# First expert pair gathered alone from unsplit rows, filler matmuls in the norms and the route, and the router's logits in another order

## The chip, the cores and the metric

The kernel runs on one core of a Trainium2 chip. The metric is device time in microseconds (us) of one launch. TensorE (PE) multiplies, PEld is its weight loading, VectorE (DVE), ScalarE (ACT) and GpSimd (POOL) do the rest, and SyncE (SP) issues the weight DMAs. TensorE's clock has two levels, 1.2 and 2.4 GHz; the profile gives it as the granted clock, 0.50 and 1.00.

## The reference

Two transformer blocks follow one another on 256 tokens of 1024 features, all in float32. The first has two layers, each a mixer, a layer norm, a mixture of experts (MoE) and a layer norm. The second is a state-space and attention mixer and a large expert lookup. The change lies around the MoE of the first block and in the norms.

```python
def grouped_moe(h, router_w, router_b, w_gate, w_up, w_down):
    logits = t @ router_w + router_b
    ...
    sel_group = jnp.argmax(group_score, axis=-1)
    ...
    top_val, top_idx = lax.top_k(masked, TOP_K)
    top_w = jax.nn.softmax(top_val, axis=-1)
    combine = jnp.sum(jax.nn.one_hot(top_idx, N_EXPERTS) * top_w[..., None], axis=1)
    for e in range(N_EXPERTS):
        hidden = jax.nn.silu(t @ w_gate[e]) * (t @ w_up[e])
        out = out + combine[:, e:e + 1] * (hidden @ w_down[e])

def first_block(...):
    for i in range(DEPTH):            # 2 layers
        ...
        x = layer_norm(ALPHA * x + (1.0 + gate) * mixer(h), ...)
        ...
        x = layer_norm(ALPHA * x + (1.0 + gate) * grouped_moe(h, ...), ...)
```

## The kernel before

Tokens lie in two tiles of 128 rows (t = 0 and 1). All matmuls go through `mm` (line 163) and all transposes through line 187, so PE's rows carry those two lines. A float32 number can be split into a rounded part and a rest (`split`, lines 151 and 153), two tiles of the type fp32r; products of split numbers are three fp32r matmuls.

A norm (`layer_norm`) works tile by tile: DVE multiplies the mixer's result by its gate (L314), adds the residual and sums (L316), ACT makes mean and variance (L320, L324, L327), POOL the inverse root (L330), and DVE normalises (L335). `warm` puts filler matmuls on PE: float32, 128x128, result unused, each reading a tile of the norm or the route, so that it runs when that tile is written. Their numbers are in the table `WA`.

A MoE follows. `logits` transposes the normalised rows in four blocks of 128 columns at a time, copies them out of PSUM (half on DVE, L194, half on ACT, L196) and multiplies them by the router's weights; a product trails its transposes by two steps (`LAG`). Both parts of `split` of the rows (fp32r) are made after each tile is normalised. `route` is a chain of some 30 small DVE operations from the logits `r_L` (L584) to the selection `r_sel` (L637); six small matmuls count and rank the selected tokens, and `hots` (L666) turns ranks into 0/1 matrices. `moe_rest` then reads the highest count into a register of every engine and branches (L828): the body runs only if an expert has more than 64 tokens. Behind the branch `moe_gather` picks, with matmuls on the split rows (two parts, two tiles, eight blocks: 32 matmuls of 256 columns), the rows of four experts, that is of two pairs; ACT and DVE scale and shift them (L767, L769). Then comes the loop over eight pairs of experts: gate and up (64 matmul records, two experts side by side), the hidden product (L730, L731), four transposes, down, and the weighted scatter into `y`. Pairs 0 and 1 are gathered in front of the loop, the next two each time in the pairs 1, 3 and 5. For each pair the `m_dT` and `m_sw` work (two transposes, two matmuls with `r_cmb`) prepares the scatter.

Weights come in pieces of 1 MB over SP's queue into 15 buffers: 12 of the streams `w` and `hl`, 3 of the pool `a`, which also holds the normalised rows and their split parts. 14 loads stand in front of the split and the 15th behind it.

What runs in which order on an engine is set by the scheduler of the tile framework; `issue_after` pins an instruction behind another.

The second block starts with `normed`: ACT squares and sums `x_mid` (L1006), DVE and POOL make the inverse root, DVE writes it on a diagonal (`rms_diag`, L1013), and 16 matmuls transpose and scale the rows.

Of the kernel before, what the change touches and what calls it, by code (L numbers as in the profile page):

```python
# [8 lines left out]
F32 = mybir.dt.float32  # L9
# [33 lines left out]
WA = {4: 3, 5: 3, 6: 3, 7: 3, (2, 0): 1, (3, 0): 3}  # L43
LAG = 2
ATR = 4
# [9 lines left out]
class Net:  # L55
# [116 lines left out]
    def warm(self, src, n=1):  # L172

        if n == 0:
            return
        pt = self.psum()
        w = src.shape[1]
        if w < WN:
            src = src[:, None, :].to_broadcast([P, WN // w, w])
            pt = pt[:, :WN].rearrange("p (a w) -> p a w", w=w)  # L180
        else:
            src, pt = src[:, :WN], pt[:, :WN]
        for _ in range(n):
            self.mm(pt, self.ones, src, True, True)
# [119 lines left out]
    def layer_norm(self, x, y, i, j):  # L304
# [4 lines left out]
        xh = self.act8().rearrange("p (t d) -> p t d", t=T)  # L309
        for t in range(T):  # L310
# [27 lines left out]
        return xh  # L338

# [220 lines left out]
    def logits(self, xh):  # L560
# [26 lines left out]
    def route(self, L):  # L587
# [61 lines left out]
        first = self.hots(0, pos)  # L649
# [12 lines left out]
    def hots(self, pr, pos):  # L662

        dt = self.t2(512, F32R).rearrange("p (t e s) -> p t e s", t=T, e=4)
        for t in range(T):
            self.nc.vector.tensor_tensor(dt[:, t], self.iota128[:, None, :CAP].to_broadcast([P, 4, CAP]),  # L666
                                         pos[:, t, 2 * pr:2 * pr + 4, None].to_broadcast([P, 4, CAP]), op=OP.is_equal)
        return [dt[:, t].rearrange("p e s -> p (e s)") for t in range(T)]

    def moe(self, i, xh, sc, sh):  # L670
        nc, V = self.nc, self.nc.vector
        L = self.logits(xh)
# [26 lines left out]
        y = self.out_tiles()  # L699
        for t in range(T):  # L700
            for hf in range(2):
                self.mm(y[t][hf].rearrange("p (a w) -> p a w", a=4), self.zerob,
                        self.zerob[:, None].to_broadcast([P, 4, P]), True, False)
# [8 lines left out]
        first = self.moe_gather(xh, sc, sh, hot, cmb, 0)  # L712
        self.phase(f"moe{i}")
        one = self.wk.tile([P, 1], F32, name="m_one", bufs=1)
        nc.scalar.activation(one, cmb[:, 0, 0:1], AF.Silu)
        xg, dT, sw = first.pop(0)
        nxt, late = first, None
        for pr in range(8):
# [46 lines left out]
    def modulate_slots(self, eng, out, in_, sc, sh, k):  # L765
        if eng == "s":
            self.nc.scalar.activation(out, in_, AF.Identity, scale=sc[:, k:k + 1], bias=sh[:, k:k + 1])  # L767
        else:
            self.nc.vector.tensor_scalar(out, in_, sc[:, k:k + 1], sh[:, k:k + 1], op0=OP.mult, op1=OP.add)  # L769

    def moe_gather(self, xh, sc, sh, d, cmb, pr):


        nc = self.nc
        xg = [self.t4().rearrange("p (k s) -> p k s", k=KB) for _ in range(2)]
        for k2 in range(KB // 2):
# [3 lines left out]
            for q in range(2):  # L780
                for kk in range(2):
                    k = 2 * k2 + kk
                    self.modulate_slots("vs"[k2 % 2], xg[q][:, k], pg[:, kk, q * P:q * P + P], sc, sh, k)
        out = []
        for q in range(2):
            dT = self.wk.tile([P, T, 128], F32R, name="m_dT", bufs=3)
            sw = self.wk.tile([P, 1], F32, name="m_sw", bufs=3)
            pw = self.psum()
            dq = [d[t][:, q * P:q * P + P].bitcast(F32) for t in range(T)]
            es = slice(2 * (pr + q), 2 * (pr + q) + 2)  # L790
            for t in range(T):
                self.transpose(pw[:, t * P:t * P + P], dq[t])
            for t in range(T):
                self.mm(pw[:, 2 * P:2 * P + 2], dq[t], cmb[:, t, es], t == 0, t == 1)
            self.evac(dT, pw[:, :2 * P].rearrange("p (t s) -> p t s", t=T))
            for e in range(2):
                r = slice(64 * e, 64 * e + 64)
                nc.vector.tensor_copy(sw[r], pw[r, 2 * P + e:2 * P + e + 1])
            out.append((xg[q], dT, sw))
        return out  # L800

    def rest_gather(self, xh, sc, sh, d, w, xg, dT, ps):

        xg = xg.rearrange("p (k s) -> p k s", k=KB)
        for half in range(2):
            pg = ps[half].rearrange("p (k s) -> p k s", k=4)
            for kk in range(4):
                self.picked(pg[:, kk], xh, half * 4 + kk, d)
# [15 lines left out]
    def moe_rest(self, xh, sc, sh, cmb, pos, cnt, w, y):  # L824

        nc, tc, V = self.nc, self.tc, self.nc.vector
        most = nc.values_load(cnt[0:1, 16:17], min_val=0, max_val=S)
        with tc.If(most > CAP):  # L828
# [5 lines left out]
            dr = self.t2(S, F32R)  # L834
# [5 lines left out]
            with tc.For_i(0, 16, 1) as e:  # L840
# [6 lines left out]
                for base in (CAP, CAP + P):  # L847
                    with tc.If(have > base):
                        for t in range(T):
                            V.tensor_scalar(d[t], self.iota128, float(base), me[:, 0, t], op0=OP.add, op1=OP.is_equal)  # L850
                            V.tensor_scalar(dw[t], d[t].bitcast(F32), me[:, 1, t], None, op0=OP.mult)
# [147 lines left out]
    def normed(self, x, gcol, hl=None):  # L999
# [878 lines left out]
```

## Time and profile before

| | us |
|---|---|
| median of three runs | 2074.36 (2067.89 to 2075.95) |
| the profiled execution, its own time | 2072.57 |
| its span, first to last instruction | 2070.8 |
| PE busy in it | 1958.4 (95%) |
| DVE, ACT, POOL busy | 1206.9, 802.1, 410.5 |

The profile gives busy time per engine, a chain of work followed back from the last instruction, and, for any stretch, the instructions in order of time. In a row of that last view the columns are start, duration, engine, line, operation, output and inputs, shape, count, and in brackets the idle time of the engine in front of it and what ended it. A float32 matmul leaves two MATMUL records (the eight products of a tile read x16), an fp32r matmul one.

### The profile page before, as it was taken

Reading aid. Unit: us, or ns where it says so; the run is one execution under the profiler, and the core shown is the slowest. Engines: PE = TensorE matmul, PEld = TensorE weight load, DVE = VectorE, ACT = ScalarE, POOL = GpSimd, SP = SyncE. Lnnn points to the kernel's source line nnn. Section 1 sums busy time; section 2 is a strip of 40 time slices with the busy share of each in tenths; the row PEclk is TensorE's granted clock in tenths of the full one; section 3 lists DMA queues with packets and bytes.
Section 4 is the critical chain, followed back from the end, with each engine's and each line's share of the span. In section 5 each row is a group of like instructions: output and inputs, shape, how many; then the busy total and the mean of one; then the engine's idle time right before and its main releaser. Section 6 shows DMA issues by size and latency. Waiting matters only on the chain.

```text
span 2070.8 us, 31874 instructions
## 1 busy us (share of the span) xinstructions
PE 1958.4 (95%) x12566; PEld 1527.3 (74%) x12567; DVE 1206.9 (58%) x2489; ACT 802.1 (39%) x1254; POOL 410.5 (20%) x319
## 2 busy tenths in 40 slices
PE   6999999989999999987988999999999999999998
PEld 4967543438898844434766889999999998888886
DVE  3554321129895422104687569767999986555555
ACT  3344111124454311113433553555444445444444
POOL 1000000002232000000231134544665550000000
PEclk9999899999999999998998999999999999999999
DMA  9797699998875699996332361544564446555564
GB/s 388 284 405 269 253 393 394 394 390 284 304 271 187 245 365 394 395 391 263 138 116 88 114 257 32 163 143 143 163 194 154 145 151 193 193 194 193 194 194 151
DMA packets 155887, 496.09 MB, mean 240 GB/s; under 512 B 10176, under 2 KB 10592, under 8 KB 147152
## 3 DMA queue, kind: packets, MB, share of 16 engines
q1 hardware_dynamic: 152880, 483.42, 65.1%
q0 software_dynamic: 2848, 10.53, 1.4%
q8 instruction: 102, 1.67, 0.3%
q14 instruction: 57, 0.47, 0.1%
HBM read 486.30 MB, written 7.61 MB: 239 GB/s over the span
## 4 chain that ended last, share of the span: by engine, by line
PE 72%; DVE 10%; ACT 2%; issue 2%; DMA 2%; POOL 1%; POOLq 0%; SPq 0%; DVEq 0%; ACTq 0%
PE ps L163 42%; PE y L163 28%; DMA w<-moe_w_down 1%; DVE pair L1553 1%; PE y L1206 1%; DVE i L1454 1%; PE ps L187 1%; DVE et L1477 1%; DVE hl L153 1%; DVE pos L1465 1%; DVE v L1453 1%; ACT hl L151 0%; DMA raw<-s_tab 0%; DVE big L1561 0%; DVE cand L1460 0%
## 5 line engine op out<-in xcount | busy, mean ns | idle before, releaser
L163 PE MATMUL ps<-hn,pair 128*128 128x256 f32 x3072 | 383.5, 285 | 4.2 <-DVE pair L1553 4.1
L163 PEld LDWEIGHTS ps<-hn,pair 128*128 128x128 f32 x3072 | 373.8, 192 | 5.6 <-DVE pair L1553 5.1
L163 PE MATMUL y<-pair,hn 128*128 128x512 f32 x1512 | 342.9, 389 | 0.0
L163 PEld LDWEIGHTS y<-pair,hn 128*128 128x128 f32 x1512 | 283.8, 188 | 59.0
L163 PE MATMUL ps<-w,t 128*64 128x512 f32 x624 | 277.3, 595 | 8.7 <-DMA w<-moe_w_down 2.8
L163 PE MATMUL ps<-hl,t 128*64 128x512 f32 x624 | 278.4, 596 | 4.5 <-DVE t L194 3.1
L1553 POOL TENSOR_TENSOR pair<-raw,pair 128x640 fp32r<-128x640 f32 x128 | 235.2, 1845 | 158.0 <-ACT pair L1551 151.8
L153 DVE TENSOR_TENSOR pair<-raw,pair 128x1024 fp32r<-128x1024 f32 x128 | 156.7, 1225 | 147.1 <-ACT pair L151 147.1
L151 ACT CAST hl<-w 128x2048 fp32r<-128x2048 f32 x79 | 150.2, 1903 | 136.6 <-PE ps L163 77.1
L151 ACT CAST pair<-raw 128x1024 fp32r<-128x1024 f32 x128 | 135.0, 1055 | 172.7 <-PE y L163 171.6
L163 PEld LDWEIGHTS ps<-w,t 128*64 128x64 f32 x624 | 81.6, 137 | 117.2 <-issue 103.8
L1551 ACT CAST pair<-raw 128x1024 fp32r<-128x1024 f32 x128 | 134.2, 1051 | 65.7 <-PE ps L163 23.9
L153 DVE TENSOR_TENSOR hl<-w,hl 128x2048 fp32r<-128x2048 f32 x51 | 119.2, 2337 | 54.2 <-ACT hl L151 51.1
L163 PE MATMUL ps<-hl,a 128*128 128x256 f32 x1008 | 129.7, 287 | 1.8 <-ACT hl L151 1.8
L163 PEld LDWEIGHTS ps<-hl,t 128*64 128x64 f32 x624 | 81.1, 137 | 67.6 <-issue 60.7
L163 PEld LDWEIGHTS ps<-hl,a 128*128 128x128 f32 x1008 | 123.9, 191 | 5.7 <-ACT hl L151 2.0
L330 POOL TENSOR_TENSOR ln_st<-ln_st,c_mhalf 128x1 f32<-128x1 f32 x8 | 6.1, 768 | 605.3 <-ACT ln_st L327 605.2
L731 DVE TENSOR_TENSOR t<-t,ps 128x512 f32<-128x512 f32 x16 | 11.0, 688 | 171.8 <-PE ps L163 171.8
L163 PE MATMUL ps<-a,hl 128*128 128x256 f32 x864 | 105.7, 284 | 1.2 <-DVE a L153 1.2
L163 PEld LDWEIGHTS ps<-a,hl 128*128 128x128 f32 x864 | 104.2, 192 | 2.6 <-DVE a L153 1.4
L163 PE MATMUL ps<-a,t 128*64 128x512 f32 (+1 forms) x352 | 100.2, 537 | 1.4 <-ACT t L196 1.4
L747 DVE SCALAR_TENSOR_TENSOR t<-ps,m_sw,t 128x512 fp32r<-128x512 f32 x32 | 24.0, 750 | 132.5 <-ACT t L746 132.0
(431 smaller groups left out, 2886.5 us busy)
## 6 DMA issues: line engine op xcount, KB each, us to landing
raw<-peer_u SPq DMA_DIRECT2D x128, 512.0 KB, 3.4
raw<-peer_v SPq DMA_DIRECT2D x128, 512.0 KB, 3.4
w<-ada_w SPq DMA_DIRECT2D x35, 1024.0 KB, 7.5
w<-moe_w_down SPq DMA_DIRECT2D x28, 1024.0 KB, 14.3
hl<-moe_w_down SPq DMA_DIRECT2D x28, 1024.0 KB, 14.2
w<-moe_w_up SPq DMA_DIRECT2D x26, 1024.0 KB, 14.2
hl<-moe_w_up SPq DMA_DIRECT2D x26, 1024.0 KB, 14.3
w<-moe_w_gate SPq DMA_DIRECT2D x24, 1024.0 KB, 14.7
```

What stands on the lines that cost most here:

```text
L151: nc.scalar.copy(hi, src)
L153: nc.vector.tensor_tensor(lo, src, hi.bitcast(F32), op=OP.subtract)
L163: self.last_mm = self.nc.tensor.matmul(out, lhsT=lhsT, rhs=rhs, start=start, stop=stop, skip_group_check=True)
L187: self.nc.tensor.transpose(out, in_, self.ident[:in_.shape[0], :in_.shape[0]])
L747: V.scalar_tensor_tensor(yl[hf], py, sw, yh[hf].bitcast(F32), op0=OP.mult, op1=OP.subtract)
L1206: self.nc.tensor.matmul(py[32 * q:32 * q + 32, :S], lhsT=self.s5_ct[ct][:, 4 * i + q], rhs=ab[q % 2][:, x, ri], start=j == 0, stop=j == 3, ...
L1453: V.max(v[:, a, rs], s)
L1454: V.max_index(ix[:, a, rs], v[:, a, rs], s)
L1465: V.max_index(pos[:, 2, rs], top[:, h, rs], cd)
L1477: V.tensor_reduce(et[:, 0:2, h], oh.rearrange("p a k j -> p a j k"), axis=AX.X, op=OP.add)
L1551: nc.scalar.copy(up[:, 0], ur)
L1553: lo = eng.tensor_tensor(up[:, 1, ks], ur[:, ks], up[:, 0, ks].bitcast(F32), op=OP.subtract)
```

## The change

`logits` finishes both products of tile 0, and puts three zeroing matmuls of `y` behind them, ahead of the transposes of tile 1. The split of the normalised rows no longer stands between the norm and the route: it is pinned behind the last scaling of the first gather, and with it the 15th weight load. The first gather takes one pair alone, with 16 float32 matmuls of 128 columns on the unsplit rows; its `m_dT` and `m_sw` work stands behind gate and up of pair 0. The other pairs are gathered two at a time in the pairs 0, 2 and 4, and pair 7 alone in pair 6, still as 32 matmuls each. The read of the count on DVE is pinned behind the 0/1 matrices. Fillers are added at the start of each norm (4 in front of a MoE, 8 behind one), behind the logits (3), in the route (5, 5, 5, 3 in place of 3 each), behind the branch (3), in the norms on the squared tile (6 in place of 3), in the last norm (6 and 4) and in `normed` (4 and 5). A filler now holds the identity (`c_pack`) and streams the tile.

```diff
-WA = {4: 3, 5: 3, 6: 3, 7: 3, (2, 0): 1, (3, 0): 3}
+WA = {4: 5, 5: 5, 6: 5, 7: 3, (2, 0): 1, (3, 0): 6}
+FILL = {"norm": (4, 8), "L": 3, "pos": 3, "x": (6, 4), "xs": (4, 5)}
+GATHER = {0: (1, (0, 1)), 2: (3, (0, 1)), 4: (5, (0, 1)), 6: (6, (1,))}
...
         for _ in range(n):
-            self.mm(pt, self.ones, src, True, True)
+            self.mm(pt, self.ident, src, True, True)
+    def fill(self, src, n):
+        with self.tc.issue_after(self.last_mm.ins):
+            self.warm(src, n)
...
     def layer_norm(self, x, y, i, j):
+        self.fill(self.ones, FILL["norm"][j])
...
             if last:
+                self.warm(x[:, t], FILL["x"][t])
...
     def logits(self, xh, idle):
-                for k in range(4):
-                    self.transpose(pt[:, k], xh[:, t, (4 * q + k) * P:(4 * q + k + 1) * P])
+                with self.tc.issue_after(self.last_mm.ins):
+                    for k in range(4):
+                        self.transpose(pt[:, k], xh[:, t, (4 * q + k) * P:(4 * q + k + 1) * P])
...
+            while late and t == 0:
+                product()
+            if t == 0:
+                with self.tc.issue_after(self.last_mm.ins):
+                    idle()
         while late:
             product()
+        self.fill(h.rearrange("p k s -> p (k s)"), FILL["L"])
...
-        first = self.hots(0, pos)
+        first = self.hots(0, pos, 2, F32)
...
     def moe(self, i, xh, sc, sh):
-        for t in range(T):
-            self.split(hl[0][:, t], hl[1][:, t], xh[:, t])
-        xh = hl
-        load()
         cmb, pos, cnt, hot = self.route(L)
...
-        first = self.moe_gather(xh, sc, sh, hot, cmb, 0)
+        self.warm(self.ones, FILL["pos"])
+        xg, got = self.first_gather(xh, sc, sh, hot)
+        with self.after(*got):
+            for t in range(T):
+                self.split(hl[0][:, t], hl[1][:, t], xh[:, t], 512)
+        xh, nxt, late = hl, [], None
+        load()
...
+            if pr == 0:
+                dT, sw = self.moe_slots(hot, cmb, 0)
-            if pr % 2 and pr + 1 < 8:
-                nxt = self.moe_gather(xh, sc, sh, self.hots(pr + 1, pos), cmb, pr + 1)
+            if pr in GATHER:
+                b, qs = GATHER[pr]
+                nxt = self.moe_gather(xh, sc, sh, self.hots(b, pos), cmb, b, qs)
...
+    def first_gather(self, x, sc, sh, d):
+        xg, last = self.t4().rearrange("p (k s) -> p k s", k=KB), [None, None]
+        for half in range(2):
+            pg = self.psum((P, 4, P))
+            for kk in range(4):
+                k = half * 4 + kk
+                for t in range(T):
+                    self.mm(pg[:, kk], x[:, t, k * P:k * P + P], d[t], t == 0, t == 1)
+            for kk in range(4):
+                k = half * 4 + kk
+                last[kk % 2] = self.modulate_slots("sv"[kk % 2], xg[:, k], pg[:, kk], sc, sh, k)
+        return xg, last
...
-        most = nc.values_load(cnt[0:1, 16:17], min_val=0, max_val=S)
+        with self.tc.issue_after(self.hot.ins):
+            most = nc.values_load(cnt[0:1, 16:17], min_val=0, max_val=S)
...
     def normed(self, x, gcol, hl=None):
+            self.warm(xs[:, t], FILL["xs"][t])
```

PE in the route of the MoE of layer 0, from the last product to the selection's matmuls; `t_1869` is a transposed block, `c_pack_66` holds the identity. Before:

```order
L163 MATMUL y<-r_W,t_1851 128x16 x4
L163 MATMUL ps<-r_L,c_ones 128x128 x3
L163 LDWEIGHTS c_zerob
L163 MATMUL y<-c_zerob 128x512
L163 MATMUL ps<-r_e,c_ones 128x128 x3
L163 MATMUL ps<-r_gm,c_ones 128x128 x3
L163 MATMUL ps<-r_m_1946,c_ones 128x128 x3
L163 MATMUL ps<-r_sel,c_ones 128x16 x2
```

After:

```order
L165 MATMUL y<-r_W,t_1869 128x16 x4
L165 MATMUL ps<-t_1869,c_pack_66 128x128 x3
L165 MATMUL ps<-r_L,c_pack_66 128x128 x5
L165 LDWEIGHTS c_zerob
L165 MATMUL y<-c_zerob 128x512
L165 MATMUL ps<-r_e,c_pack_66 128x128 x5
L165 MATMUL ps<-r_gm,c_pack_66 128x128 x5
L165 MATMUL ps<-r_m_1964,c_pack_66 128x128 x3
L165 MATMUL ps<-r_sel,c_ones 128x16 x2
```

The fillers in front of the selection's matmuls go from 12 to 21; the zeroing matmul stays among them.

DVE in the norm in front of the MoE of layer 1, from the second tile's sum to the logits. Before:

```order
L316 SCALAR_TENSOR_TENSOR a,ln_st<-x_mid,a 128x1024
L557 TENSOR_TENSOR r_B<-ps,c_pack_106 128x16
L335 TENSOR_SCALAR a<-a,ln_st 128x1024
L194 COPY t_5990<-ps 128x512
L153 TENSOR_TENSOR a<-a 128x1024
L335 TENSOR_SCALAR a<-a,ln_st 128x1024
L194 COPY t_6004<-ps 128x512
L153 TENSOR_TENSOR a<-a 128x1024
L584 TENSOR_TENSOR r_L<-y,r_B 128x32
```

After:

```order
L324 SCALAR_TENSOR_TENSOR a,ln_st<-x_mid,a 128x1024
L573 TENSOR_TENSOR r_B<-ps,c_pack_106 128x16
L344 TENSOR_SCALAR a<-a,ln_st 128x1024 x2
L201 COPY t_6023<-ps 128x512
L201 COPY t_6051<-ps 128x512
L608 TENSOR_TENSOR r_L<-y,r_B 128x32
```

The two subtractions of the split are gone, and the copy of tile 0's transposes now stands behind the normalising of both tiles.

PE in the expert loop of the MoE of layer 0, from the end of the up projection of pair 0 to its first down matmul; `t_2365` and `t_2320` are its hidden product. Before:

```order
L163 MATMUL ps<-hl,t_2255 64x512
L187 MATMUL ps<-c_pack_66,t_2365 128x128 x4
L163 MATMUL ps<-w,t_2369 64x512
```

After:

```order
L165 MATMUL ps<-hl,t_2241 64x512
L194 MATMUL ps<-c_pack_66,t_1994 128x128 x2
L165 MATMUL ps<-r_cmb,t_1994 128x2 x2
L165 MATMUL ps<-t_2323,a 128x256 x32
L194 MATMUL ps<-c_pack_66,t_2323 128x128 x2
L165 MATMUL ps<-r_cmb,t_2323 128x2 x2
L194 MATMUL ps<-c_pack_66,t_2323 128x128 x2
L165 MATMUL ps<-r_cmb,t_2323 128x2 x2
L194 MATMUL ps<-c_pack_66,t_2320 128x128 x4
L165 MATMUL ps<-w,t_2401 64x512
```

The gather of pairs 1 and 2 and the scatter's preparation for pairs 0 to 2 now stand between up and the hidden transposes. In the whole loop the hidden transposes stood right behind up in the pairs 0, 4, 6 and 7 before, and do so in the pairs 3, 5 and 7 now; in the others a gather or a scatter lies between, in whole or in part.

## Rows read from the trace of the kernel before

**Rows 1.** Stretches: length, busy time (instructions) of PE, PEld, DVE, ACT, POOL; granted clock, DMA share, GB/s.

```profile
195.10:224.34 29.24, 24.66 (x144) 22.38 (x142) 16.40 (x64) 10.61 (x21) 0.80 (x3) 0.71 0.58 221
224.34:458.20 233.86, 221.63 (x1041) 94.04 (x1044) 43.14 (x91) 34.19 (x66) 0.00 (x0) 1.00 1.01 386
...
696.40:722.51 26.11, 23.68 (x155) 22.09 (x154) 16.85 (x64) 10.32 (x21) 1.39 (x1) 0.80 0.67 251
...
957.00:970.30 13.30, 2.13 (x9) 1.68 (x9) 11.29 (x17) 8.99 (x14) 2.98 (x4) 0.69 1.01 409
970.30:976.60 6.30, 6.30 (x33) 6.20 (x33) 2.65 (x7) 2.86 (x7) 0.05 (x1) 0.56 0.73 286
```

**Rows 2.** PE's waits in the expert loop of layer 0: sum, count, longest.

```profile
PE ps L187 <- DVE t L731: 3.6, 5, 0.9
...
PE ps L163 <- DMA w<-moe_w_down: 1.4, 2, 0.7
```

**Rows 3.** Order of time, logits of layer 0's MoE.

```profile
198.52 1.96 PE L163 MATMUL y<-r_W,t 128*128 128x16 f32 x16 [0.65 <-DVE t L194]
...
200.32 0.81 PE L163 MATMUL y<-c_zerob 128*128 128x512 bf16 x3
...
200.86 0.81 DVE L335 TENSOR_SCALAR a<-a,ln_st 128x1024 f32<-128x1024 f32 x1 [1.26 <-POOL ln_st L330]
...
202.78 1.23 DVE L153 TENSOR_TENSOR a<-a 128x1024 fp32r<-128x1024 f32 x1 [1.11 <-ACT a L151]
...
203.93 0.68 DVE L194 COPY t<-ps 128x512 f32<-128x512 f32 x1
...
204.66 3.60 PE L163 MATMUL y<-r_W,t 128*128 128x16 f32 x16 [0.97 <-DVE t L194]
208.30 0.19 DVE L584 TENSOR_TENSOR r_L<-y,r_B 128x32 f32<-128x32 f32 x1 [3.69 <-PE y L163]
```

**Rows 4.** The products of tile 1 as a stretch, as in Rows 1.

```profile
204.66:208.26 3.60, 3.60 (x16) 3.49 (x16) 0.00 (x0) 0.96 (x1) 0.00 (x0) 0.50 1.02 406
```

**Rows 5.** Order of time, route and first gather of layer 0's MoE.

```profile
211.69 1.49 PE L163 MATMUL ps<-r_gm,c_ones 128*128 128x128 f32 x6
...
212.76 0.19 DVE L637 TENSOR_TENSOR r_sel<-r_o,r_o 128x32 f32<-128x32 f32 x1
...
212.97 1.49 PE L163 MATMUL ps<-r_m,c_ones 128*128 128x128 f32 x6
...
214.04 0.82 PEld L163 LDWEIGHTS ps<-r_sel,c_ones 128*128 128x128 f32 x4
...
215.26 0.37 PE L163 MATMUL ps<-r_sel,c_pack 128*128 128x16 f32 x2
...
216.72 0.47 PE L163 MATMUL ps<-t,a 128*128 128x256 f32 x2 [1.09 <-DVE t L666]
...
217.56 0.43 DVE L666 TENSOR_TENSOR t<-c_pack,r_pos 128x256 fp32r<-128x256 f32 x1 [1.03 <-DVEq L828]
```

**Rows 6.** Order of time, layer 1's MoE.

```profile
700.25 0.69 DVE L194 COPY t<-ps 128x512 f32<-128x512 f32 x1 [0.75 <-PE ps L187]
...
712.11 0.19 DVE L637 TENSOR_TENSOR r_sel<-r_o,r_o 128x32 f32<-128x32 f32 x1
...
713.21 0.53 PEld L163 LDWEIGHTS ps<-r_sel,c_ones 128*128 128x128 f32 x4
...
714.13 0.37 PE L163 MATMUL ps<-r_sel,c_pack 128*128 128x16 f32 x2
```

**Rows 7.** Order of time, PE in the expert loop, pair 1.

```profile
261.41 3.14 PE L163 MATMUL ps<-t,a 128*128 128x256 f32 x24
...
267.21 0.38 PE L187 MATMUL ps<-c_pack,t 128*128 128x128 f32 x2
...
268.41 0.63 PE L187 MATMUL ps<-c_pack,t 128*128 128x128 f32 x4
```

**Rows 8.** Order of time, the start of the second block.

```profile
970.30 6.53 PE L163 MATMUL ps<-rms_diag,x_mid 128*128 128x128 f32 x32 [6.25 <-DVE rms_diag L1013]
```

More of the change, by code (lines that the diff above doesn't have):

```diff
@@ L338, in layer_norm, with after @@
         return xh
+    def after(self, *ops):
+        stack = ExitStack()
+        for op in ops:
+            stack.enter_context(self.tc.issue_after(op.ins))
+        return stack
     def behind(self):
@@ L558, in router, with logits @@
         self.r_wb = w, b
-    def logits(self, xh):
+    def logits(self, xh, idle):
         w, b = self.r_wb
@@ L671, in moe, with zeros @@
         nc, V = self.nc, self.nc.vector
-        L = self.logits(xh)
+        y = []
+        def zeros(n):
+            for _ in range(n):
+                y.append(self.acc.tile([P, 512], F32, name="y"))
+                self.mm(y[-1].rearrange("p (a w) -> p a w", a=4), self.zerob,
+                        self.zerob[:, None].to_broadcast([P, 4, P]), True, False)
+        L = self.logits(xh, lambda: zeros(3))
         wg = self.io["moe_w_gate"][i].rearrange("e (k p) n -> e p k n", p=P)
@@ L693, in moe @@
         hl = [self.act8(F32R).rearrange("p (t d) -> p t d", t=T) for _ in range(2)]
-        for t in range(T):
-            self.split(hl[0][:, t], hl[1][:, t], xh[:, t])
-        xh = hl
-        load()
         cmb, pos, cnt, hot = self.route(L)
[L699 to L703, printed above, removed]
+        zeros(1)
+        y = [y[:2], y[2:]]
         def scatter(pr, yh, yl, dT):
@@ L711, in moe @@
         self.moe_rest(xh, sc, sh, cmb, pos, cnt, (wg, wu, wd), y)
[L712 to L713 removed]
         one = self.wk.tile([P, 1], F32, name="m_one", bufs=1)
         nc.scalar.activation(one, cmb[:, 0, 0:1], AF.Silu)
[L716 to L717 removed]
+        self.warm(self.ones, FILL["pos"])
+        xg, got = self.first_gather(xh, sc, sh, hot)
+        self.phase(f"moe{i}")
+        with self.after(*got):
[3 more added lines that the diff above has]
+        load()
         for pr in range(8):
@@ L766, in modulate_slots, with moe_gather @@
         if eng == "s":
[L767 to L775, printed above, removed]
+            return self.nc.scalar.activation(out, in_, AF.Identity, scale=sc[:, k:k + 1], bias=sh[:, k:k + 1])
+        return self.nc.vector.tensor_scalar(out, in_, sc[:, k:k + 1], sh[:, k:k + 1], op0=OP.mult, op1=OP.add)
+    def first_gather(self, x, sc, sh, d):
[10 more added lines that the diff above has]
+        return xg, last
+    def moe_gather(self, xh, sc, sh, d, cmb, pr, qs=(0, 1)):
+        xg = [self.t4().rearrange("p (k s) -> p k s", k=KB) for _ in qs]
         for k2 in range(KB // 2):
@@ L779, in moe_gather, with moe_slots @@
                 self.picked(pg[:, kk], xh, 2 * k2 + kk, d)
-            for q in range(2):
+            for j, q in enumerate(qs):
                 for kk in range(2):
                     k = 2 * k2 + kk
[L783 to L800, printed above, removed]
+                    self.modulate_slots("vs"[k2 % 2], xg[j][:, k], pg[:, kk, q * P:q * P + P], sc, sh, k)
+        return [(x, *self.moe_slots([a[:, q * P:q * P + P] for a in d], cmb, pr + q)) for x, q in zip(xg, qs)]
+    def moe_slots(self, d, cmb, pr):
+        dT = self.wk.tile([P, T, 128], F32R, name="m_dT", bufs=3)
+        sw = self.wk.tile([P, 1], F32, name="m_sw", bufs=3)
+        pw = self.psum()
+        d = [a if a.dtype == F32 else a.bitcast(F32) for a in d]
+        for t in range(T):
+            self.transpose(pw[:, t * P:t * P + P], d[t])
+        for t in range(T):
+            self.mm(pw[:, 2 * P:2 * P + 2], d[t], cmb[:, t, 2 * pr:2 * pr + 2], t == 0, t == 1)
+        self.evac(dT, pw[:, :2 * P].rearrange("p (t s) -> p t s", t=T))
+        for e in range(2):
+            r = slice(64 * e, 64 * e + 64)
+            self.nc.vector.tensor_copy(sw[r], pw[r, 2 * P + e:2 * P + e + 1])
+        return dT, sw
     def rest_gather(self, xh, sc, sh, d, w, xg, dT, ps):
@@ L807, in rest_gather @@
             for kk in range(4):
-                self.picked(pg[:, kk], xh, half * 4 + kk, d)
+                k = half * 4 + kk
+                for t in range(T):
+                    self.mm(pg[:, kk], xh[:, t, k * P:k * P + P], d[t], t == 0, t == 1)
             for kk in range(4):
```

13 lines of the change are left out of this document (7 added, 6 removed).

## The prediction

> **What bounds the kernel now.** I read the stretches first [rows 1]. In the expert loop of layer 0 PE is busy 221.63 of 233.86 us at full clock, and I take layer 1's loop, the same code, as alike. The DMA is full too (share 1.01), yet PE's waits there name weights for only 1.4 us, and the largest entry is the hidden transposes waiting for DVE's hidden product, 3.6 us in five waits [rows 2]. So inside the loop PE is the bound, and every matmul that is put there costs its own duration unless it falls into one of those waits. The two stretches ahead of the loops, 29.24 and 26.11 us with clocks of 0.71 and 0.80, are chains of dependent small steps, and so is the way from the last norm of the first block into the second, 13.30 us with PE busy 2.13, and 6.30 us at a clock of 0.56 behind it [rows 1]. The change works on these, and pays in the loops. The reader should keep the two currencies apart: a chain is shortened by taking steps out of it or by a higher clock, the loop only by less PE work.
>
> The profiled execution took 2072.57 us, 1.79 below the median of the runs. The sum is made against the former, and 1.8 is added at the end.
>
> **A filler's price.** Two groups of three fillers start at 211.69 and 212.97 at the low clock [rows 5]: 1.28 us, 0.427 each, so 0.213 at 2.4 GHz, twice the rate. The same holds for any float32 matmul of 128 columns: the 16 that open the second block took 6.53 us, 0.408 each, at a mean clock of 0.56 [rows 8].
>
> **Logits of layer 0.** Before, DVE copies tile 1's first transposes only at 203.93, because the split's subtraction stands ahead of it until 204.01; then the 16 product records take 3.60 us at half clock, and `r_L` starts at 208.30. Tile 0's products start at 198.52 and take 1.96 [rows 3]. Now the subtraction is gone. The added fillers at the norm's start delay tile 0's transposes by some four fillers at the rate between the two, about 1.0 us, so tile 0's products run from 199.5 to 201.5, the zeroing (0.81, less an overlap as before) to 202.1, tile 1's transposes behind it by order to 203.0, its last copy (0.68, overlapped by half) to 203.4, and its products, 1.96 at full clock, to 205.4. `r_L` comes at about 205.5 instead of 208.3: **-2.8**. If the products stay at half clock, 1.64 of that is lost; the bounds are -1.2 and -2.8.
>
> **Route of layer 0.** The selection is written at 212.76 and ready near 212.95, but PE loads it only at 214.04, behind three fillers on `r_m` [rows 5]. From `r_L` to that point are 4.65 us of DVE's chain, unchanged. The new order has 21 fillers and one zeroing in this stretch: 21 x 0.213 is 4.5, with the zeroing 4.7. They fit the chain to 0.1 us only at full clock; then the selection starts at once: **-1.1**. At half clock they take 9.0, 4.3 more than the chain, which is the slow end.
>
> **First gather of layer 0.** From the last selection matmul's end (215.26 + 0.37 = 215.63) to the first gate matmul at 224.34 are 8.71 us [rows 5, 1]: ranks and 0/1 matrix to 216.72, a second 0/1 matrix that waited behind the branch 1.03 us, 32 gather matmuls, and the scatter's preparation. Now: the same 1.1 to the branch with both matrices ahead of it (DVE's read of the count is pinned behind them; each is half as wide as the 0.43 us one before, so the pin costs what one full matrix cost), three fillers 0.64, 16 float32 matmuls 16 x 0.213 = 3.4, and nothing else, 5.1: **-3.6**. No row shows float32 matmuls in this role; the nearest for the same number of result values are the fp32r gather matmuls in the loop, 24 in 3.14 us [rows 7], so 4.2 for 32. Upper bound 4.2, at half clock 6.8; I take 3.4, since the fillers have exactly this shape and type.
>
> Here the Trainium skill speaks against the change: "FP8 and Floating Point Precision", TensorE Precision Notes, says that true float32 takes four passes through the array. By that rule the 16 matmuls stream as much as the 32 fp32r ones of twice the width, so the pair gathered alone would save none of the 4.2 us; at the loop's rate it adds 0.8 per layer, 1.6 in all. The filler's 0.213 already contains such passes, and I stay with it.
>
> **Expert loop, each layer.** It gets a fourth gather of 32 matmuls, 4.2 us, and two more preparations for the scatter, from 267.21 to 268.41 = 1.2 [rows 7], which stood ahead of it before. What can it hide in? The five waits for the hidden product sum to 3.6 [rows 2]. By the order, pair 0's and pair 4's or 6's are now covered by gathers, but pairs 3 and 5, covered before, are open now: one wait of 0.7 (3.6 / 5) fewer. So +4.2 + 1.2 - 0.7 = **+4.7**. Bounds: 0, if the loop goes by something other than PE, and +5.4, if no wait is covered. The split itself (two ACT casts and two DVE subtractions, 1.23 us each in [rows 3]) moves beside pair 0's gate and up; DVE is busy 43 of 234 us there, so it costs nothing unless the hidden product of pair 0 waits behind it, at most 2.5. The 15th weight load, on SP's queue, moves past SP's own read of the count and its branch and behind the first gather; it comes later by the whole route, with 14 pieces ahead of it and the next loads behind it (the last rival).
>
> **Layer 0 in all:** -2.8 - 1.1 - 3.6 + 4.7 = -2.8.
>
> **Layer 1.** DVE now normalises tile 1 before it copies tile 0's transposes, which it took up at 700.25 [rows 6], and 11 fillers (4, 1 and 6) stand ahead of those transposes: 11 x 0.213 = 2.3 us, 1.3 of it inside idle time as before. Logits **+1.0**. Route: `r_sel` is ready at 712.30, PE starts at 713.21, **-0.9** [rows 6]. Gather: from 714.50 to 722.51, 8.01 us, to 5.1: **-2.9** [rows 6, 1]. Loop **+4.7**. In all +1.9.
>
> **The clock in the logits.** Before, PE was busy 3.60 of 3.60 us with products of 16 columns and the clock stayed at 0.50 [rows 4]. So a busy PE alone did not raise it there, and the new logits are again a run of such products with thin spots: I allow **+1.0** for one stretch at the low level. The Trainium skill ("TensorE: Matmul & The Clock Gate", Part 1) says that the throttled state is the default and that activity releases it. By that rule fillers are activity and the allowance falls away; the row of 204.66 shows no release under full busyness, so I keep it.
>
> **Into the second block.** Between 957.00 and 970.30 the chain runs on ACT, DVE and POOL, and PE is idle 11.2 us [rows 1]. 34 fillers now stand there (8, 1, 6, 10 and 9): 7.2 us at full clock, which the idle time hides; at half clock 14.5, 3.3 too long. The 16 matmuls behind them go from 6.53 to 16 x 0.23 (0.408 x 0.56) = 3.7: **-2.8**. Bounds -2.8 and +3.3; I take the first because most of the fillers are ready long before the chain ends. What comes next there is the projection's first weights; DMA share is 1.01 in that stretch, so a few tenths may be given back.
>
> **The rest.** The norm behind layer 0's MoE gets 11 fillers more, with DVE's normalising as the later end: 0, at most three fillers at 0.427 = 1.3. In the second block's other `normed` five fillers (1.07) stand behind the last square, in front of the diagonal matmuls: **+0.3**, bounds 0 and 1.1.
>
> **Sum.** -2.8 + 1.9 + 1.0 - 2.8 + 0.3 = -2.4: 2070.2 for a profiled execution, 2072.0 as a median.
>
> **The rivals.**
> - *Half clock in the route (slower).* The clock was 0.71 and 0.80 on the mean in the fronts [rows 1]. If it is at 1.2 GHz when the fillers behind the logits issue, 21 of them outlast the chain by 4.3 and the 16 gather matmuls take 3.4 more: +7.7 per layer. One layer gives 2079.7, both 2087.4. It decides as soon as the fillers take more than 0.22 each. For it speaks [rows 4]; against it, that 21 wide matmuls in a row are more than the route ever had.
> - *The stream of weights sets the loop's length (faster).* The DMA share is 1.01 in the loop [rows 1]. Then the extra gather is free and the loops stay as long as they were: -9.4, 2062.6. Against it: 1.4 us of waits for weights in 234 [rows 2].
> - *The clock doesn't follow the fillers at the second block.* The -2.8 isn't there: 2074.8. Here the change doesn't do what it says.
> - *A late weight.* 14 instead of 15 pieces are loaded ahead; at 386 GB/s one piece of 1 MB is 2.7 us [rows 1]. If the loop runs out of them once in each layer: +5.4, 2077.4. Against it: the waits in [rows 2] are short with the 15th landing well ahead.
>
> **How the numbers follow.** Forecast 0.46, with its own range of 2068 to 2076; half clock in one layer 0.10, in both 0.05; the stream 0.17; no clock at the second block 0.14; a late weight 0.08. A measurement of this kernel can tell about 0.5% from no change, 10.4 us: faster is below 2064.0, slower above 2084.7. The stream's case reaches below the bound, and so does the forecast where its copy and clock terms all fall well: 0.23. Slower needs both layers at half clock, or one and a late weight: 0.07. The range 2061 to 2080 takes in the stream's case and half clock in one layer, and leaves out 0.15 or so.
>
> **What would show it.** `r_L` of layer 0 some 10.4 us after the mixer's last matmul (13.2 before); PE's first selection matmul right behind `r_sel`; 5.1 us from the last selection matmul to the first gate matmul; expert loops of about 238.6 us with 229 busy; the diagonal matmuls in 3.7 us; a granted clock of 1.00 in both routes. A loop of 234 would show the stream's case, a clock of 0.50 in the route the first rival, a wait for `moe_w_gate` or `moe_w_up` the last. The forecast is wrong in its core if the front keeps its length: then the gain I book there was the clock's, not the order's.

## The result and the profile after

The changed kernel takes 2089.36 us as a median of four runs (2082.36 to 2091.71), the kernel before 2072.70 in the same measurement. The ratio is 1.0082, 95% interval 1.0057 to 1.0107: about 17 us slower, where 2072 was forecast. The profiled execution is the fastest of the four (2082.36, span 2080.6, against 2072.57 and 2070.8 before), so its stages explain some 10 us; where the other 7 lie in the other executions no profile shows.

The stretches of the changed kernel, with columns as in [rows 1]: layer 0's front, its expert loop, layer 1's mixer, layer 1's front, its loop, the way into the second block.

```profile
193.93:222.08 28.15, 22.65 (x168) 21.54 (x167) 11.40 (x53) 7.03 (x13) 0.80 (x3) 0.88 0.51 192
222.08:459.71 237.63, 225.46 (x1083) 98.18 (x1083) 49.12 (x106) 38.02 (x72) 0.00 (x0) 1.00 1.01 383
472.72:703.26 230.54, 221.79 (x1699) 201.16 (x1699) 173.52 (x309) 102.71 (x148) 57.32 (x62) 1.00 0.72 256
703.26:732.28 29.02, 23.97 (x182) 22.84 (x180) 11.16 (x52) 7.03 (x13) 0.55 (x1) 0.88 0.50 191
732.28:969.92 237.64, 225.47 (x1083) 98.14 (x1083) 49.40 (x106) 37.76 (x71) 0.00 (x0) 1.00 0.99 375
969.92:985.99 16.07, 12.16 (x101) 11.29 (x100) 13.50 (x24) 9.82 (x20) 2.39 (x4) 1.00 0.76 297
```

Two of these answer to stretches of before that the prediction didn't read, the mixer of layer 1 and its loop:

```profile
470.79:696.57 225.78, 224.51 (x1685) 201.31 (x1684) 173.40 (x307) 102.78 (x146) 58.61 (x62) 1.00 0.74 259
722.50:957.00 234.50, 221.61 (x1037) 93.88 (x1036) 43.10 (x91) 32.02 (x64) 0.00 (x0) 1.00 0.97 365
```

Layer 0's front is hardly shorter than in [rows 1] (28.15 us for 29.24) and layer 1's is longer (29.02 for 26.11), although the clock is better (0.88 for 0.71 and 0.80). The loops are 3.8 and 3.1 us longer, and PE's busy time in each grew by 3.8 (225.46 for 221.63 in layer 0). The mixer, which the diff doesn't touch, is 4.8 us longer.

What fills the front is seen in the order of time on PE behind the last selection matmul, which ends at 210.06 in layer 0. The rows of layer 0, then the one of layer 1:

```profile
209.68 0.38 PE L165 MATMUL ps<-r_sel,c_pack 128*128 128x16 f32 x2
214.87 1.62 PE L165 MATMUL ps<-c_ones,c_pack 128*128 128x128 f32 x6 [4.81 <-PEq L875]
...
216.28 5.87 PE L165 MATMUL ps<-t,a 128*128 128x128 f32 x32
...
726.53 1.62 PE L165 MATMUL ps<-c_ones,c_pack 128*128 128x128 f32 x6 [3.86 <-PEq L875]
```

PE sits 4.81 and 3.86 us at its own branch (L875; PEq is PE's sequencer). Before, 1.09 us passed there, and the row names the 0/1 matrix as the releaser [rows 5]. PE's compare-and-branch itself lasts 4.32 and 3.39 us by its start and end in the trace, 0.44 and 0.42 before. Behind it layer 0's fillers run at a granted clock of 0.50 and the gather at 0.61 on the mean (5.87 us). In the DMA queues between 210.1 and 214.8 there is nothing but instruction blocks (packets, MB, share):

```profile
q8 instruction: 1, 0.02, 2.4%
q14 instruction: 4, 0.03, 2.3%
```

So the first suspicion: the branch's target isn't there, and PE waits for its code. By itself this view doesn't show it. The kernel before has the same blocks behind its branch, between 215.8 and 218.2, where PE works on:

```profile
q14 instruction: 4, 0.03, 4.8%
q8 instruction: 1, 0.02, 2.7%
```

The difference is that the changed kernel has one more block on q8 behind the wait (215.2), and the one in the wait lands at 212.99, 1.6 us before PE goes on. That q8 carries PE's code is seen from its size: 102 such blocks, 1.67 MB, in the whole kernel before, for 25,133 matmuls and weight loads; no other engine runs a tenth of that.

### The profile page after: what moved, and what is told of

Read it like the earlier page. It is cut to its first block, busy times and chain, and to the rows that moved or that the text cites. A ratio compares the mean times of both kernels' runs of the same rounds, so it can differ in the third digit from the quotient of the medians.

```text
span 2080.6 us, 32385 instructions
## 1 busy us (share of the span) xinstructions
PE 1971.0 (95%) x12806; PEld 1546.7 (74%) x12807; DVE 1211.2 (58%) x2497; ACT 802.6 (39%) x1254; POOL 408.7 (20%) x319
## 4 chain that ended last, share of the span: by engine, by line
PE 54%; DVE 8%; ACT 2%; issue 1%; DMA 0%; SPq 0%; POOL 0%; POOLq 0%; DVEq 0%; ACTq 0%
PE ps L165 29%; PE y L165 24%; PE y L1254 1%; DVE i L1502 1%; DVE hl L155 1%; DVE pair L1601 1%; DMA c_swap<-swap 0%; DVE v L1501 0%; DVE et L1525 0%; DVE ps L1247 0%; DVE pos L1513 0%; ACT hl L153 0%; DVE cand L1508 0%; DVE s L1504 0%; DVE ps L1242 0%
```

## The experiments

Each kernel was compared with the kernel before on the same chip. Stage times below are differences between events of one profiled execution: the mixer's last matmul, `r_L`, the last selection matmul, the first gate matmul, the last scatter matmul, the first projection. "Built order" is the order of instructions in the program.

**A shorter body behind the branch (a_short).** On the changed kernel:

```diff
-                for base in (CAP, CAP + P):
+                for base in (CAP,):
```

> The changed kernel with a shorter body behind the branch: of an expert's tokens the part beyond 192 is left out there; the body doesn't run with these inputs, so the work done is the same. On PE the jump from the branch to the code behind the body is 235 instructions instead of 434. Theory A (the 4.81 and 3.86 us in front of the first fillers behind the branch are PE's code being fetched, since the target lies beyond the blocks of 256 instructions that are already there): both waits fall to about 0.5 us beyond the ranks, the clock stays up, the first gather takes 3.4 us in both layers; 10 us less than the changed kernel, some 2079 as a median. Theory B (the branch waits for PE's queue of fillers, or for the later read of the count): no change, 2089 and waits of 4 to 5 us.

Measured: 2081.19, ratio 1.0038 (1.0024 to 1.0052), 9 us less than the changed kernel by the ratios (some 6 either way by their intervals). Not one instruction that runs is different. PE in layer 0, then layer 1:

```profile
214.11 0.91 PE L165 MATMUL ps<-c_ones,c_pack 128*128 128x128 f32 x6 [0.85 <-PEq L875]
215.05 3.84 PE L165 MATMUL ps<-t,a 128*128 128x128 f32 x32
...
722.99 0.91 PE L165 MATMUL ps<-c_ones,c_pack 128*128 128x128 f32 x6 [0.76 <-PEq L875]
723.75 3.84 PE L165 MATMUL ps<-t,a 128*128 128x128 f32 x32
```

The wait at the branch is gone and the gather runs at full clock. From the last selection matmul to the first gate matmul are 5.56 and 5.29 us, 10.8 less in the two layers together. (The two profiled executions differ by only 1.5 us in all: in that of a_short the route of layer 0, the mixer and the second block took longer.) Theory B, by which the fillers or the pinned read hold the branch, is out: both are still here.

**A longer body in the kernel before (b_long).**

```diff
+                        for _ in range(11):
+                            self.transpose(ps[2][:, :P], hid[:, :P])
                         hv = self.moe_hidden_t(hid, ps[2], hT)
```

> The kernel before with eleven more transposes in each half of the body behind the branch, which does not run with these inputs: the jump is 478 instead of 434 instructions. Theory A, with a block of 256 instructions fetched ahead: layer 0's branch stays within the block that is there (493 of 512), layer 1's does not (523): layer 0 as before, layer 1's first gather matmul 3 to 4 us later, 2076 to 2078 as a median. Theory B: code that never runs changes nothing, 2073.

Measured: 2078.14, ratio 1.0021 (1.0012 to 1.0031). Code that never runs costs 4 us. The first gather matmuls of both layers:

```profile
218.74 5.52 PE L163 MATMUL ps<-t,a 128*128 128x256 f32 x32 [4.00 <-PEq L828]
...
718.20 6.53 PE L163 MATMUL ps<-t,a 128*128 128x256 f32 x32 [4.03 <-PEq L828]
```

Layer 0's branch waits too, which was not expected: the limit lies lower than 512. The branch's place in the built program gives a rule. The jump is the number of PE's instructions from the branch to its target: 434 with the whole body, 235 with the short one, 478 in b_long. The place is counted from a point that recurs every 256 instructions; this offset is fitted, and of the 256 possible ones only it and its neighbour separate the branches that wait from the quick ones in all twelve kernels. Place plus jump is:

| kernel | layer 0: sum, wait in the branch | layer 1 |
|---|---|---|
| before | 449, 0.44 us | 435, 0.42 |
| changed | 515, 4.32 | 689, 3.39 |
| a_short | 316, 0.35 | 291, 0.41 |
| b_long | 493, 3.36 | 523, 3.48 |
| va | 316, 0.35 | 480, 2.12 |
| v1 | 304, 0.44 | 401, 0.33 |
| e1_full | 437, 0.44 | 477, 0.33 |

The five other kernels have sums of 250 to 451 and waits of 0.22 to 0.46. Up to 477 the branch is quick, at 480 it waits 2.12 us, from 493 on 3.36 to 4.32. In layer 1 of e1_full, at 477, the wait comes a little later, behind the first two gather matmuls, and the row names no releaser:

```profile
712.15 0.47 PE L165 MATMUL ps<-t,a 128*128 128x256 f32 x2 [1.05 <-DVE t L692]
715.17 5.28 PE L165 MATMUL ps<-t,a 128*128 128x256 f32 x30 [2.55 <-issue]
```

By the packets' times in the traces, all six of these waits, five in branches and this one, end 1.3 to 1.6 us after a block on q8 has landed. In layer 1 of va that block had set out 0.34 us before the branch, in the other five 0.9 to 1.6 us after it; by that, the 2.12 us there are the same wait with a head start. The rule agrees with the Trainium skill ("Runtime: NRT & Kernel Launch", Instruction fetch mechanics), by which code comes in blocks of 256 instructions, and a taken branch whose target isn't in the current window of two blocks has to fetch it. The two blocks would be 512; the runs put the limit for the target between 477 and 480.

**The old gather with all fillers (va).** On a_short:

```diff
+        for t in range(T):
+            self.split(hl[0][:, t], hl[1][:, t], xh[:, t])
+        load()
         cmb, pos, cnt, hot = self.route(L)
...
-        xg, got = self.first_gather(xh, sc, sh, hot)
+        first = self.moe_gather(xh, sc, sh, hot, cmb, 0)
```

> As a_short (body cut in the same way), but the gather as before: split rows in front of the route, two pairs gathered ahead of the loop, gathers in the pairs 1, 3 and 5. If the new gather only trades 3.6 us in front of the loop for 3.5 in it, the time is that of a_short within 3 us. If the loop hides the fourth gather, this one is 6 us slower than a_short; if the first gather saves less than the loop pays, it is 3 to 7 us faster.

Measured: 2086.15, ratio 1.0059 (1.0042 to 1.0076). That is 4.4 us slower than a_short by the ratios, not far from the 6 by which the expectation would have called the fourth gather hidden; the stages say otherwise. The loops are 234.38 and 233.73 here against 237.68 and 237.65 in a_short: the fourth gather costs 3.3 and 3.9 us, and as PE's busy time differs by as much (221.74 here, 225.50 there in layer 0), it is not hidden. From the last selection matmul to the first gate matmul are 7.01 us in layer 0 (5.56 in a_short) and 9.85 in layer 1, of which some 1.7 are the wait at the branch; behind it the clock is 0.50, and the three fillers take 1.62 us for 0.91. Layer 0's logits take 13.59 us, with the split's subtraction among them, against 10.05. By stages the new gather gains 1.7 us in layer 0 and loses 1.0 in layer 1, or more without the low clock that va has there; as far as it goes it is an exchange, as the prediction had it.

**Without the fillers added behind the MoE and behind the branch (v1).** On va, in both layers, and with the squared tile's fillers back at 3:

```diff
-WA = {4: 5, 5: 5, 6: 5, 7: 3, (2, 0): 1, (3, 0): 6}
-FILL = {"norm": (4, 8), "L": 3, "pos": 3, "x": (6, 4), "xs": (4, 5)}
+WA = {4: 5, 5: 5, 6: 5, 7: 3, (2, 0): 1, (3, 0): 3}
+FILL = {"norm": (4, 0), "L": 3, "pos": 0, "x": (6, 4), "xs": (4, 5)}
```

> As va, and without the added fillers in the norm behind layer 0's MoE and behind the branch (0 and 3 in place of 8 and 6 there). In the built order the mixer of layer 1 then stands as in the kernel before. If that order is what the changed kernel loses in the mixer (4.8 us between the first projection and the last, PE waiting for DVE's product with the decay), this is 5 to 7 us faster than va, near 2064 to 2068 as a median; if the loss there comes from something else, such as later weight loads, the mixer takes as long as in va.

Measured: 2075.98, ratio 1.0007 (0.9995 to 1.0019), 10.8 us less than va, where 5 to 7 were expected; the 2064 to 2068 were missed, as va itself came out slower. Of the 10.8 the mixer has 8.5; another 2 are layer 1's first gather, since its branch has moved to a sum of 401 and no longer waits. The mixer, va first, then v1:

```profile
471.30:705.62 234.32, 224.81 (x1699) 203.77 (x1699) 172.88 (x309) 102.29 (x148) 59.26 (x62) 0.99 0.71 250
```

```profile
470.26:696.03 225.77, 224.49 (x1685) 201.30 (x1684) 173.34 (x307) 102.72 (x146) 58.62 (x62) 1.00 0.75 259
```

**Eight fillers alone (b_f8).** On the kernel before, with the body cut:

```diff
+        if (i, j) == (0, 1):
+            with self.tc.issue_after(self.last_mm.ins):
+                self.warm(self.ones, 8)
         for t in range(T):
             st = self.wk.tile([P, 4], F32, name="ln_st")
```

> The kernel before with one thing added: eight fillers at the start of the norm behind layer 0's MoE, where PE is idle for some 4 us (the body behind the branch is cut as in a_short and doesn't run; both branches stay within the blocks that are there). In the built order these eight are enough to turn the mixer of layer 1 into the changed kernel's order, with the background matmuls (y from c_rep) in runs of 31 and 24 rather than spread. If that order is the loss: the mixer takes 230 to 234 us instead of 225.8, and the median is 2079 to 2083. If the mixer's loss in the changed kernel comes from what arrives late there (weights, the decay table) because of the new gather, this kernel is within 2 us of the one before, 2072 to 2076.

Measured: 2082.18, ratio 1.0053 (1.0036 to 1.0070), 11 us slower. The mixer takes 236.86, 11.1 more (230 to 234 were expected): eight matmuls in another stage account for all of it through an order that they change. PE in the built order behind the first projection of the mixer, in the kernel before and in the changed one (`c_rep` marks matmuls of the background work; the pairs of `t` are a head's score products, which need a product made by DVE):

```
before                                  changed
y<-w,c_rep 32x256 x3                    y<-w,c_rep 32x256
ps<-hl,a 128x256 x48                    ps<-hl,a 128x256 x48
y<-w,c_rep 32x256 x12                   y<-w,c_rep 32x256 x31
ps<-t_3821,t_3819 128x256 x2            ps<-t_3846,t_3844 128x256 x3
```

And what PE waits for in the mixer, first in the changed kernel, then in b_f8 (L1022 and L978 are DVE's product for the scores, L988 and L944 ACT's copy of a head's values):

```profile
PE ps L165 <- DVE t L1022: 4.2, 2, 2.8
PE ps L165 <- ACT t L988: 3.3, 2, 2.1
```

```profile
PE ps L163 <- ACT t L944: 5.6, 2, 3.4
PE ps L163 <- DVE t L978: 2.7, 1, 2.7
```

The kernel before and v1 have neither wait. In b_f8 the two are 8.3 of the 11.1 us; the rest is PE's busy time (227.28 for 224.51), at a mean clock of 0.97. The order of time in the changed kernel shows who is late:

```profile
505.67 1.90 ACT L153 CAST hl<-w 128x2048 fp32r<-128x2048 f32 x1 [5.50 <-PE ps L165]
505.68 3.65 PE L165 MATMUL y<-w,c_rep 128*32 128x256 f32 x62
...
507.60 2.50 DVE L162 TENSOR_TENSOR hl<-w,hl 128x512 fp32r<-128x512 f32 x4 [3.42 <-ACT hl L153]
...
510.01 0.55 DVE L1022 TENSOR_TENSOR t<-ps,t 128x384 f32<-128x384 f32 x1
...
510.71 1.53 PE L165 MATMUL ps<-t,t 128*128 128x256 f32 x6 [1.38 <-DVE t L1022]
```

DVE splits the next weights for 2.50 us ahead of the small product, ACT ahead of that for 1.90, and PE has already spent 31 background matmuls in one go. In the kernel before they stood in portions of 3, 12 and 16 between the heads, with the small product earlier on DVE.

**No added fillers (m3).** On a_short, the numbers of all fillers as in the kernel before (the table `WA` goes back, too).

```diff
-FILL = {"norm": (4, 8), "L": 3, "pos": 3, "x": (6, 4), "xs": (4, 5)}
+FILL = {"norm": (0, 0), "L": 0, "pos": 0, "x": (0, 0), "xs": (0, 0)}
```

> a_short without any filler that the change adds (those of the kernel before stay): the logits' order, the new gather, the split behind it. If the fillers are worth what their places show, the way into the second block is 3 us longer than in a_short, the first gathers run at half clock for a part (+2 each), the mixer keeps its new order: 2086 to 2090. If the fillers are worth nothing, 2081 as a_short.

Measured: 2082.77, ratio 1.0046 (1.0029 to 1.0063), not to be told from a_short. The new logits and gather turn the mixer's order without any added filler (235.21 us). By stages the fillers give 2.1 us into the second block (18.14 without, 16.07 with) and 2.0 in layer 0's logits (12.00, 10.05); the expectation of 5 us and more is a miss, partly since layer 0's loop, 235.37, is 2.3 shorter here, for which I have no cause.

**Towards a faster one (d5, e1, e1_full).** The old gather, fillers chosen for each norm so that the mixer's background work stays spread, the split's subtraction on POOL:

```diff
+            with self.tc.issue_after(self.pw.ins):
+                for q in range(0, D, 512):
+                    nc.gpsimd.tensor_tensor(hl[1][:, t, q:q + 512], xh[:, t, q:q + 512], ...)
...
+        self.fill(self.ones, {(0, 0): 8, (1, 0): 0, (0, 1): 0, (1, 1): 8}[i, j])
```

> The logits' order and the fillers of the changed kernel in front of the MoE (8 instead of 4), in the route and towards the second block, none in the norm behind layer 0's MoE and none behind the branch; the gather and its place as before; the split's subtraction on POOL instead of DVE, its rounding on ACT between the two tiles' copies; the body behind the branch cut as in a_short. The mixer's background matmuls stay spread in the built order. By the terms measured so far: logits -2.5, route and gather -1, loops 0, mixer 0, layer 1 -1, towards the second block -3: 2066 to 2069. If POOL's subtractions hold up the first gather or DVE's small steps, the route and gather of each layer are 2 to 4 us longer and it comes out at 2072 to 2076.

Measured: 2070.05, ratio 0.9991 (0.9981 to 1.0001). The mixer keeps 226.8, but layer 0's loop takes 241.10 and layer 1's front, up to the first gather matmul, is at a clock of 0.65:

```profile
218.52:459.62 241.10, 225.57 (x1057) 95.36 (x1060) 46.22 (x96) 35.42 (x66) 0.00 (x0) 0.98 1.01 382
696.23:720.80 24.57, 23.21 (x130) 21.39 (x128) 10.84 (x51) 8.00 (x13) 5.49 (x5) 0.65 0.58 222
```

Four fillers more in layer 1's norm, (1, 0): 4, make e1:

> As d5, with four fillers also at the start of the norm in front of layer 1's MoE, where d5 had none and its clock stood at 0.50 from 699 to 716 (logits 14.77 us, route 8.74, against 11.07 and 6.86 before). The body behind the branch is cut as in a_short. If the clock there follows the fillers, layer 1's logits and route are 4 to 6 us shorter than in d5; the first loop loses its 7 us again only if they belong to the built order and not to that one execution: 2060 to 2066 as a median. If the low clock there was a matter of POOL's subtractions, it stays at 2070.

Measured: 2071.41, ratio 0.9989 (0.9980 to 0.9998). The same stretch of layer 1's front falls from 24.57 to 19.75 us at a clock of 0.91, as expected. The first loop keeps 239.34, with PE's waits as in d5 (4.7 us for the hidden product and 4.6 for the scaled one, L786; 3.6 and 1.4 in the kernel before), so that loss comes with the kernel and not with one execution. The median doesn't follow the front, and why not is open. With the body whole and 87 one-column matmuls at the start, which move PE's code by 174 instructions (e1_full):

```diff
+    pt = net.psum()
+    for _ in range(87):
+        net.mm(pt[:, :1], net.zerob, net.zerob[:, :1], True, True)
```

> e1 with the whole body behind the branch (434 instructions of PE) and 87 matmuls of one column at the program's start, which move PE's code by 174 instructions, so that the targets lie at 437 (layer 0) and 477 (layer 1), counted from the start of the block of the branch as in the runs before, where 449 was there and 480 half, 493 not at all. Layer 0's branch costs nothing; layer 1's costs nothing, too, if the limit is above 477, else up to 3 us. 2062 to 2068, and faster than the kernel before in full.

Measured: 2071.83, ratio 0.9991 (0.9982 to 1.0001). Neither branch waits, and layer 0's first gather is as quick as in e1 (8.11 and 8.06 us). In layer 1 the wait of 2.55 us shown above stands behind the branch, and its first gather takes 10.46 us for 7.82 in e1; that expectation held for the branch alone. So e1, with the body cut, is some 2 us faster than the kernel before, and nothing here does better; e1_full, which keeps all of the computation, can't be told from the kernel before. The three expectations (2066 to 2069, 2060 to 2066, 2062 to 2068) forecast more than was gained.

**The change without its side effects (g3).** The new gather, the new logits and the fillers on the route, with the norms' fillers so chosen that the mixer's order stays spread, and the body cut:

```diff
+        self.fill(self.ones, {(0, 0): 0, (1, 0): 4, (0, 1): 0, (1, 1): 8}[i, j])
```

> The changed kernel without its two side effects: new gather, split behind it, new logits' order, fillers in the route and towards the second block, body cut as in a_short (both branches then find their code), and no added fillers in the norm in front of layer 0's MoE, in the norm behind it and behind the branch (4 in front of layer 1's MoE, as in the change); with these numbers the built order keeps the mixer's background matmuls spread. If code fetch and the mixer's order are all that turned the gain into a loss, the stages of the change show as in a_short (gather about 5 us from the last selection matmul, loops 237.6, the way into the second block about 16 to 17) with the mixer at 226: 2067 to 2071, where a_short has 2081. If something else belongs to the new gather, 2076 or more.

Measured: 2071.94, ratio 0.9995 (0.9986 to 1.0004). Both branches are quick, the mixer takes 228.13 and the loops 237.64 each. That is a microsecond above the expected 2067 to 2071. The first gathers take 6.96 and 6.28 us and the way into the second block 17.58, each 1 to 1.5 more than in a_short; the mixer still has 2.4 more than in the kernel before, 0.7 of it a wait for DVE's product for the scores and 1.7 PE's busy time.

## Why the prediction was wrong

It held that the time is the sum of what the diff touches. Its own terms came out near; two costs stood outside them. In us against the kernel before, by stages:

| term | forecast | changed kernel | a_short |
|---|---|---|---|
| logits, layer 0 | -2.8 | -3.1 | -3.1 |
| route, layer 0 | -1.1 | -1.3 | +0.3 |
| first gather, layer 0 | -3.6 | +3.3 | -3.1 |
| loop, layer 0 | +4.7 | +3.8 | +3.8 |
| norm behind it | 0 | +0.4 | +1.5 |
| mixer, layer 1 | none | +4.8 | +7.9 |
| logits, layer 1 | +1.0, and +1.0 for the clock in either layer | +0.7 | +0.7 |
| route, layer 1 | -0.9 | +0.8 | -0.8 |
| first gather, layer 1 | -2.9 | +1.6 | -2.7 |
| loop, layer 1 | +4.7 | +3.1 | +3.1 |
| into the second block | -2.8 | -3.5 | -3.5 |
| start, and the second block to its last matmul | +0.3 | -1.1 | +4.1 |

The last line is not the change's: from its first projection to its last matmul, the second block takes 1085.0 us in the profiled execution of before and 1090.7 in that of b_long, which has the same instructions there. It differs between executions, and I assign none of it.

**Failed: "the same 1.1 to the branch".** In the first gather's term I carried the branch's price over from [rows 5] as if it belonged to the branch. It belongs to where the code lies. The wait was 4.81 and 3.86, and after it PE ran layer 0's fillers and gather at a low clock, 7.2 us instead of 4.7; the terms of -3.6 and -2.9 came out as +3.3 and +1.6. Shown by a_short and b_long from both sides; 9 us of the 17 by the ratios. The Trainium skill ("Runtime: NRT & Kernel Launch", Instruction fetch mechanics) states the rule, and I had not weighed it. None of my rivals had the branch; half clock in the route prices only the slow gather that follows it.

**Failed: what isn't touched stays.** Layer 1's mixer had no term in the sum; it took 4.8 us more, and 7.9 in a_short. The built order was read in three places before the run, none in the mixer. The scheduler that orders the program answers to small changes far away: eight fillers in a norm cost 11 us in the next mixer. Shown by b_f8, and by v1 against va. The built orders before and after already differed there in runs of 12 against 31 background matmuls, so it was to be read before the run. What makes the scheduler choose one order or the other is open; fillers alone (b_f8), all fillers with the old gather (va) and the new logits and gather without added fillers (m3) all turn it.

**Sized about right.** Logits, route at full clock, first gather once the branch finds its code (5.6 and 5.3 measured in a_short for 5.1, 3.8 of it the float32 matmuls for the row's 3.4), second block (-3.5 for -2.8; the diagonal matmuls now start and end in two halves with a wait of 0.41 between):

```profile
981.75 2.02 PE L165 MATMUL ps<-rms_diag,x_mid 128*128 128x128 f32 x16 [0.20 <-DVE rms_diag L1061]
984.19 2.05 PE L165 MATMUL ps<-rms_diag,x_mid 128*128 128x128 f32 x16 [0.41 <-DVE a L1067]
```

The Trainium skill ("FP8 and Floating Point Precision", TensorE Precision Notes) gives true float32 four passes through the array. The estimate by it, 4.2 for the gather's float32 matmuls, is as near to the measured 3.8 as the row's 3.4.

The loops cost 3.8 and 3.1 for 4.7. Two sizes in that term were off and partly made up for each other: PE's busy time grew by 3.83 us in layer 0, where 4.2 and 1.2 had been added, and the five waits for the hidden product grew from 3.6 to 4.3 us, where 0.7 had been taken off. The allowance for the clock in the logits wasn't needed (the products of tile 1 ran in 1.96 us in both layers); in layer 1 the clock fell in the route, to 0.61 between 716 and 720, which is its +0.8.

**The rivals.** Half clock in the route did not happen in layer 0 (1.00) and happened for some 4 us in layer 1. The free extra gather did not happen: PE's busy time and the loop grew together. Late weights did not happen: no weight stands among PE's waits in either loop. The fillers that don't reach the second block did not happen: the granted clock there is 1.00. With both side effects removed, g3 takes 2071.9 against a forecast of 2072.0; that the figure is met so exactly is luck, since its terms are not the forecast's (layer 0's logits -1.0 for -2.8, its first gather -1.8 for -3.6, the mixer +2.4 for nothing). But the balance is shown: without the two side effects, and with some fillers fewer, the change lies between 0.14% faster and 0.04% slower.

## What to carry to other kernels

Where a program has a branch over code that seldom runs, that code's length and the number of instructions ahead of it are part of the time: shorten the body or shift it. Look at the releaser of the first instruction behind the branch, and for an idle time without a releaser some instructions later. Before trusting a sum over the parts of a diff, compare the built order over the whole program, above all where one engine covers for another. A gain of some microseconds in a chain is worth little where the same change puts as much into a stretch that PE bounds.

## What the hardware showed that I had not expected

A wait of 3.4 to 4.3 us in a branch, ending 1.3 to 1.6 us after a block of PE's code has landed, and 2.12 in the one case where the block had set out before the branch. Eleven transposes in each half of code that doesn't run cost 4 us. And 4.8 us of idle PE at the branch let the clock fall to 0.50 for the fillers and most of the gather behind it: the gather took 5.87 us, 3.84 at full clock.
